# A row normalisation with four unequal buffers and a first tile stored in halves

## Chip, cores, metric

The kernel runs on one core of one Trainium2 chip. The metric is device time in microseconds (us). Each kernel was run several times, and medians, ranges and ratios are of these runs. A ratio is the mean time of one kernel's fast runs over the mean time of the fast runs of the kernel before that were made in the same rounds on the same chip, so it is not quite the ratio of the medians that stand beside it, which are of all runs. A run that lies over 1.5% above the fastest of its kernel counts as slow; there were two, and both were profiled (sizes_only and halves_six).

## The reference

```python
x: (32, 512, 1024) float32
sums = np.sum(np.abs(x), axis=-1, keepdims=True)
return (x / (sums + 1e-8)).astype(np.float32)
```

There are 16,384 rows of 1024 numbers. Each row is read once, summed, scaled and written once: 67.1 MB in and 67.1 MB out.

## The kernel before

The rows are dealt to 128 partitions, 128 rows to each, and moved in tiles of 12 rows a partition (the last has 8). Within a tile the rows of one partition are neighbours in memory, so each partition's part is one contiguous line of 48 KB.

```python
R = 12
BUFS = 4
...
def piece(flat, i):
    a, k = P * sum(rows[:i]), rows[i]
    return flat[a : a + P * k, :].rearrange("(p r) d -> p r d", p=P)

sbuf = ctx.enter_context(tc.tile_pool(name="sbuf", bufs=BUFS))
...
for i, k in enumerate(rows):
    x_tile = sbuf.tile([P, R, d], FP32)
    nc.sync.dma_start(out=x_tile[:, :k, :], in_=piece(x_flat, i))
    normalize(x_tile, 0, k, k // 2)
    nc.scalar.dma_start(out=piece(out_flat, i), in_=x_tile[:, :k, :])
```

`normalize` runs one reduce over all rows on VectorE, two tiny operations, then a multiply of half of the rows on VectorE and an activation for each row of the other half on ScalarE, all in place. SyncE issues the loads and ScalarE the stores. A load waits until the store that used its buffer four tiles earlier has landed.

Of the kernel before, what the change touches and what calls it, by code (L numbers as in the profile page):

```python
# [1 line left out]

# [4 lines left out]

FP32 = mybir.dt.float32
EPS = 1e-8


@with_exitstack
def kernel(
    ctx: ExitStack,
    tc: tile.TileContext,
    x: bass.AP,
    out: bass.AP,
):
    nc = tc.nc
    P = nc.NUM_PARTITIONS  # L20

    x_flat = x.flatten_outer_dims()
    out_flat = out.flatten_outer_dims()
    n, d = x_flat.shape


    R = 12
    BUFS = 4
    per_partition = n // P
    assert n % P == 0  # L30
    rows = [R] * (per_partition // R)
    if per_partition % R:
        rows.append(per_partition % R)

    def piece(flat, i):
        a, k = P * sum(rows[:i]), rows[i]
        return flat[a : a + P * k, :].rearrange("(p r) d -> p r d", p=P)

    sbuf = ctx.enter_context(tc.tile_pool(name="sbuf", bufs=BUFS))
    stats = ctx.enter_context(tc.tile_pool(name="stats", bufs=4))  # L40

    def normalize(x_tile, r0, k, kv):

        s = stats.tile([P, R], FP32)
        nc.vector.tensor_reduce(  # L45
            out=s[:, :k],
            in_=x_tile[:, r0 : r0 + k, :],
            axis=mybir.AxisListType.X,
            op=mybir.AluOpType.add,
            apply_absolute_value=True,  # L50
        )
        nc.vector.tensor_scalar_add(out=s[:, :k], in0=s[:, :k], scalar1=EPS)  # L52
        inv = stats.tile([P, R], FP32)
        nc.vector.reciprocal(out=inv[:, :k], in_=s[:, :k])  # L54
        nc.vector.tensor_mul(  # L55
            out=x_tile[:, r0 : r0 + kv, :],
            in0=x_tile[:, r0 : r0 + kv, :],
            in1=inv[:, :kv].unsqueeze(2).to_broadcast([P, kv, d]),
        )
        for r in range(kv, k):  # L60
            row = x_tile[:, r0 + r, :]
            nc.scalar.activation(  # L62
                out=row,
                in_=row,
                func=mybir.ActivationFunctionType.Copy,
                scale=inv[:, r : r + 1],
            )

    with tc.manual_schedule():
        for i, k in enumerate(rows):  # L70
            x_tile = sbuf.tile([P, R, d], FP32)
            nc.sync.dma_start(out=x_tile[:, :k, :], in_=piece(x_flat, i))  # L72
            normalize(x_tile, 0, k, k // 2)
            nc.scalar.dma_start(out=piece(out_flat, i), in_=x_tile[:, :k, :])  # L74


# [1 line left out]
_INS = ['x']  # L78
_OUTS = [((32, 512, 1024), 'float32')]


# [23 lines left out]
```

## Time and profile before

| | before |
|---|---|
| time, median (range) | 317.77 us (317.46 to 318.05, 6 runs) |
| span of the profiled run | 315.8 us |
| VectorE busy | 212.4 us, 67% |
| mean DMA rate over the span | 425 GB/s |
| rate in the middle | 430 to 437 GB/s |

The kernel is a stream with the DMA as its bound. The page's DMA row and the rate say that; the prediction below shows these lines and reads them. How a DMA's work is split matters later: each transfer is carried by 16 DMA engines, eight lines each. Each line is one packet in the trace, with its start, duration and size. The trace's list of packets doesn't name the engine, but on one engine a packet starts as the last one ends (3 to 4 ns before its end), so most engines can be followed from packet to packet.

### The profile page before, as it was taken

How to read it: one execution, taken by the hardware profiler on the slowest of the kernel's cores; microseconds unless marked ns; L12 is line 12 of the kernel's file. 1: busy time of each engine (PE TensorE's matmuls, PEld its weight loads, DVE VectorE, ACT ScalarE, POOL GpSimd, SP SyncE). 2: the span in 40 equal slices, each digit the busy share in tenths (PEclk: the TensorE clock that was granted, in tenths of full speed). 3: DMA queues.
4: the chain of work that ended last, by engine and by line, in shares of the span. 5: the costliest groups of instructions: out<-in, count | busy, mean ns of one | idle time of the engine just before them, and what ended most of it. 6: DMA issues, size and time to landing. Idle time of an engine off the chain costs nothing.

```text
span 315.8 us, 227 instructions
## 1 busy us (share of the span) xinstructions
DVE 212.4 (67%) x44; ACT 69.0 (22%) x65; POOL 0.2 (0%) x4
## 2 busy tenths in 40 slices
DVE  0069999998499079719944991797099449949300
ACT  0010804308007000700440070007003400701300
POOL 0000000000000000000000000000000000000000
DMA  8999999999999999999999999999999999999996
GB/s 311 467 417 411 467 367 442 405 454 430 417 448 430 423 461 423 436 442 417 442 442 411 449 436 411 448 436 423 448 430 436 442 413 450 421 448 417 448 403 278
DMA packets 3169, 134.23 MB, mean 425 GB/s; under 512 B 352, under 2 KB 352, under 8 KB 352
## 3 DMA queue, kind: packets, MB, share of 16 engines
q1 hardware_dynamic: 1584, 67.11, 49.8%
q10 hardware_dynamic: 1584, 67.11, 49.1%
q14 instruction: 1, 0.01, 0.0%
HBM read 67.11 MB, written 67.11 MB: 425 GB/s over the span
## 4 chain that ended last, share of the span: by engine, by line
DMA 55%; DVE 25%; another core or an unknown queue 9%; ACT 4%; issue 0%; SPq 0%; DVEq 0%; ACTq 0%
DMA x_tile<-in_x_dram 41%; DVE s L45 19%; DMA out_dram<-x_tile 14%; DVE x_tile L55 6%; ACT x_tile L62 4%; DVE inv L54 0%; DVE s L52 0%; SPq L72 0%; DVEq L54 0%; ACTq L74 0%
## 5 line engine op out<-in xcount | busy, mean ns | idle before, releaser
L45 DVE TENSOR_REDUCE s<-x_tile 128x12 f32<-128x12288 f32 (+1 forms) x11 | 138.2, 12564 | 81.1 <-DMA x_tile<-in_x_dram 81.1
L62 ACT ACTIVATE x_tile<-x_tile,inv 128x1024 f32<-128x1024 f32 x64 | 67.7, 1135 | 207.6 <-DVE inv L54 207.6
L55 DVE TENSOR_TENSOR x_tile<-x_tile,inv 128x6144 f32<-128x6144 f32 (+1 forms) x11 | 70.0, 6364 | 0.4
L62 ACT ACT_TABLE_LOAD x1 | 1.3, 1283 | 18.4 <-DMA x_tile<-in_x_dram 18.4
L54 DVE RECIPROCAL inv<-s 128x12 f32<-128x12 f32 (+1 forms) x11 | 2.5, 226 | 0.9
L52 DVE TENSOR_SCALAR s<-s 128x12 f32<-128x12 f32 (+1 forms) x11 | 1.9, 173 | 0.4
L89 POOL MEMSET const-bfloat16-1.0<- 128x1 bf16 x1 | 0.1, 101 | 0.0
L89 POOL MEMSET const-uint8-127<- 128x1 uint8 x1 | 0.1, 101 | 0.0
L89 POOL MEMSET const-float32-0.0<- 128x1 f32 x1 | 0.1, 98 | 0.2 <-issue 0.2
L89 POOL MEMSET const-float32-1.0<- 128x1 f32 x1 | 0.1, 98 | 0.0
## 6 DMA issues: line engine op xcount, KB each, us to landing
x_tile<-in_x_dram SPq DMA_DIRECT2D x10, 6144.0 KB, 38.5
out_dram<-x_tile ACTq DMA_DIRECT2D x10, 6144.0 KB, 53.5
x_tile<-in_x_dram SPq DMA_DIRECT2D x1, 4096.0 KB, 33.7
out_dram<-x_tile ACTq DMA_DIRECT2D x1, 4096.0 KB, 19.5
```

What stands on the lines that cost most here:

```text
L45: nc.vector.tensor_reduce(out=s[:, :k], in_=x_tile[:, r0 : r0 + k, :], axis=mybir.AxisListType.X, op=mybir.AluOpType.add, apply_absolute_v ...
L52: nc.vector.tensor_scalar_add(out=s[:, :k], in0=s[:, :k], scalar1=EPS)
L54: nc.vector.reciprocal(out=inv[:, :k], in_=s[:, :k])
L55: nc.vector.tensor_mul(out=x_tile[:, r0 : r0 + kv, :], in0=x_tile[:, r0 : r0 + kv, :], in1=inv[:, :kv].unsqueeze(2).to_broadcast([P, kv, d]),)
L62: nc.scalar.activation(out=row, in_=row, func=mybir.ActivationFunctionType.Copy, scale=inv[:, r : r + 1],)
L89: nc = _bacc.Bacc("TRN2", target_bir_lowering=False, num_devices=1)
```

## The change

The intent is to keep more bytes in flight (51 rows instead of 48) and to begin storing earlier.

```diff
-    R = 12
-    BUFS = 4
+    R = 16
+    SLOTS = [R, 12, 12, 11]
...
+    while left:
+        rows.append(min(left, SLOTS[len(rows) % len(SLOTS)]))
+        left -= rows[-1]
...
-    sbuf = ctx.enter_context(tc.tile_pool(name="sbuf", bufs=BUFS))
+    slots = [
+        ctx.enter_context(tc.tile_pool(name=f"slot{b}", bufs=1))
+        for b in range(len(SLOTS))
+    ]
...
-            x_tile = sbuf.tile([P, R, d], FP32)
+            x_tile = slots[i % len(SLOTS)].tile([P, SLOTS[i % len(SLOTS)], d], FP32)
             nc.sync.dma_start(out=x_tile[:, :k, :], in_=piece(x_flat, i))
-            normalize(x_tile, 0, k, k // 2)
-            nc.scalar.dma_start(out=piece(out_flat, i), in_=x_tile[:, :k, :])
+            h = k if i else k // 2
+            for r0 in range(0, k, h):
+                normalize(x_tile, r0, h, h // 2)
+                nc.scalar.dma_start(
+                    out=piece(out_flat, i)[:, r0 : r0 + h, :],
+                    in_=x_tile[:, r0 : r0 + h, :],
+                )
```

More of the change, by code (lines that the diff above doesn't have):

```diff
@@ L24 @@
     n, d = x_flat.shape
-    R = 12
-    BUFS = 4
-    per_partition = n // P
+    R = 16
+    SLOTS = [R, 12, 12, 11]
     assert n % P == 0
-    rows = [R] * (per_partition // R)
-    if per_partition % R:
-        rows.append(per_partition % R)
+    left = n // P
+    rows = []
+    while left:
+        rows.append(min(left, SLOTS[len(rows) % len(SLOTS)]))
+        left -= rows[-1]
     def piece(flat, i):
```

## The prediction

> **What bounds the kernel now.** I read the page's slices first, to see which resource is full, then the queues and issues, then stretches of the span, and last the chain of waits and the timeline for the edges. The program is pure streaming: 128 rows of 4096 B in each of 128 partitions, in and out.
>
> ```profile
> DVE 212.4 (67%) x44; ACT 69.0 (22%) x65; POOL 0.2 (0%) x4
> ...
> DMA  8999999999999999999999999999999999999996
> ...
> DMA packets 3169, 134.23 MB, mean 425 GB/s; under 512 B 352, under 2 KB 352, under 8 KB 352
> ...
> x_tile<-in_x_dram SPq DMA_DIRECT2D x10, 6144.0 KB, 38.5
> out_dram<-x_tile ACTq DMA_DIRECT2D x10, 6144.0 KB, 53.5
> x_tile<-in_x_dram SPq DMA_DIRECT2D x1, 4096.0 KB, 33.7
> ```
>
> The DMA row is 9 in 38 of 40 slices; only the first and the last are lower. VectorE is idle for a third of the span. The same by stretches (start:end, length, busy times, clock, DMA share, GB/s):
>
> ```profile
> 0.00:8.00 8.00, 0.00 (x0) 0.00 (x0) 0.20 (x4) 1.00 0.83 307
> ...
> 60.00:80.00 20.00, 18.11 (x4) 6.34 (x6) 0.00 (x0) 1.00 1.01 435
> ...
> 200.00:240.00 40.00, 30.88 (x5) 6.34 (x6) 0.00 (x0) 1.00 1.00 433
> 240.00:280.00 40.00, 28.05 (x8) 12.69 (x12) 0.00 (x0) 1.00 1.00 433
> 280.00:300.00 20.00, 13.48 (x4) 4.27 (x4) 0.00 (x0) 1.00 1.00 435
> 300.00:308.00 8.00, 0.00 (x0) 0.00 (x0) 0.00 (x0) 1.00 0.93 401
> 308.00:316.00 8.00, 0.00 (x0) 0.00 (x0) 0.00 (x0) 1.00 0.63 270
> ```
>
> From 60 to 300 us the rate is 433 to 435 GB/s. 134.2 MB at 433 take 310.0 us, so of the 315.8 us span only 5.8 are not full-rate transfer: about 2.8 at the start (the first 100 us move 42.1 MB, which is 97.2 us' worth) and 3.0 at the end. The measured 317.85 us are 2.0 more than the span. The chain of waits names DMA for 55% and VectorE for 25%, but it follows single tiles; the reduces in it are no bound, because other tiles' transfers fill the DMA meanwhile. These lines of the timeline show it (start, length, engine, and in brackets the idle time before and what ended it):
>
> ```profile
> 18.35 12.95 DVE L45 TENSOR_REDUCE s<-x_tile 128x12 f32<-128x12288 f32 x1 [18.35 <-DMA x_tile<-in_x_dram]
> 38.45 0.37 ACTq L74 DMA_DIRECT2D out_dram<-x_tile  x1
> 58.38 0.34 ACTq L74 DMA_DIRECT2D out_dram<-x_tile  x1
> 83.26 12.95 DVE L45 TENSOR_REDUCE s<-x_tile 128x12 f32<-128x12288 f32 x1 [5.05 <-DMA x_tile<-in_x_dram]
> 112.19 12.95 DVE L45 TENSOR_REDUCE s<-x_tile 128x12 f32<-128x12288 f32 x1 [8.91 <-DMA x_tile<-in_x_dram]
> 257.23 12.95 DVE L45 TENSOR_REDUCE s<-x_tile 128x12 f32<-128x12288 f32 x1 [8.91 <-DMA x_tile<-in_x_dram]
> 281.44 8.69 DVE L45 TENSOR_REDUCE s<-x_tile 128x8 f32<-128x8192 f32 x1 [4.13 <-DMA x_tile<-in_x_dram]
> 295.18 0.34 ACTq L74 DMA_DIRECT2D out_dram<-x_tile  x1
> ```
>
> The first four loads (48 rows) are all issued by 3 us and would alone keep the DMA busy to 2.8 + 48 x 1.211 = 60.9 us (a row of all partitions is 524,288 B, 1.211 us at 433 GB/s). The first store joins at 38.45, so there is no hole before it. At the end, the last load lands at 281.4 and its store is issued at 295.18, but SyncE's closing waits (the stretches 280 to 293 and 293 to 310; us in total, times, longest) show when the two stores before it land:
>
> ```profile
> SPq L100 <- DMA out_dram<-x_tile: 42.5, 1, 42.5
> SPq L100 <- DMA out_dram<-x_tile: 14.5, 1, 14.5
> ```
>
> The first of these waits began after SyncE's last load issue at 247.7, so it ended near 290.3, and the second near 305: older stores cover the last computation, and the last store has some 10 us in hand.
>
> **What the Trainium skill says.** "DMA: Bandwidth & Descriptors", section "Where 436 GB/s comes from", gives 435.2 GB/s as the limit of the ports; the trace's 433 to 435 agrees, so the steady stretch has nothing left. The same page, "Queues, rings and completion order", says that each DMA engine takes turns between its queues, one packet at a time. The trace agrees, and shows what a packet is here: 3169 = 22 transfers x 16 engines x 9 + 1, thus eight data packets (one partition's contiguous rows each) and a small one per engine. The last load has 8-row packets beside stores of 12-row ones: it took 257.2 to 281.4, 24.2 us or 20.0 rows, which is 8 + 12. An equal share of bytes would give 16 rows, 19.4 us. So one load and one store advance in step, packet by packet, and a pair costs the sum of their rows. "VectorE: DVE Perf Modes", section "The perf-mode tier table", has the reduce at one element per cycle at any type; 12,288 elements at the page's 0.96 GHz are an estimated 12.80 us, and 12.95 is measured, so row counts scale its cost linearly.
>
> **The change part by part.** Tiles become 16, 12, 12, 11, 16, 12, 12, 11, 16, 10 rows: 10 instead of 11. Bytes are the same. Buffers hold 51 rows instead of 48. Loads fall from 11 to 10; stores stay at 11, since tile 0 is stored as 8 + 8. VectorE keeps 44 instructions and the same elements; one row costs (12.95-8.69)/4 = 1.066 us in the reduce and (6.56-4.42)/2 = 1.066 in the multiply. From the start of the reduce to the store's issue: 20.1 us for 12 rows (38.45-18.35), 13.7 for 8 (295.18-281.44); worked out from these, 26.5 for 16, 18.8 for 11, 16.9 for 10. Everything hangs on whether the DMA ever has both queues empty, so I walk through it, with data taken to end 1 us before landing (first load: 2.8 + 12 x 1.211 = 17.3 against the landing at 18.33), and 2 us from issue to first byte.
>
> Start. Load 0 now has 16 rows: 2.8 + 19.4, landing at 23.2 instead of 18.3. The first half's store is issued at 23.2 + 13.7 = 36.9, the second at 50.6, tile 1's at 70.6, tile 2's at 90.5. So halving wins 1.5 us against 38.45 for the first store, with 8 rows in it instead of 12: the larger tile eats what the halves give. By 58.4 us the old kernel had offered 24 rows, the new one 16. Loads alone would last to 2.8 + 51 x 1.211 = 64.6, well past 36.9: no hole here either.
>
> Hand-over. The first store of the old kernel needed about 5 us to get its turn; with that, half 0a is moved from about 42 in step with eight load packets (8 + 11.6 rows) to 66, half 0b with load 3's last five (11.9 rows) to 80, then alone to 84. Only then is the 16-row buffer free, and load 4 goes out near 85 (old: 73.7). The load queue is empty from about 80 to 87: the one new wait. But tile 1's store, queued since 70.6, keeps the engines full there. Cost: 0.
>
> Steady part, each pair as the sum of rows x 1.211: load 4 lands near 121, load 5 at 150, load 6 at 179, load 7 at 211, load 8 at 245. Each next load is issued 4 to 6 us before the previous has ended, where the old kernel had 9.6; a late one costs nothing while a store is queued. Stores are issued 12 to 33 us before their turn (store 4 ready at 148, its turn at 172; store 7 ready at 230, its turn at 265). VectorE needs 79 to 85 us per cycle of 51 rows, while the DMA needs 2 x 51 x 1.211 = 123.5. No hole.
>
> End. Load 9 lands near 271; tile 8's 26.5 us end at about the same time, so VectorE is just free. Store 8 is issued at 271.4, when store 7 still has 11 us to go; store 9 at 288.2, when store 8 goes on to 300.5. Both have about 10 us in hand, as before. Last data at 2.8 + 256 x 1.211 = 312.8, plus the old tail.
>
> Sum: removed from the path 0, added 0; the floor of 310.0 + 2.8 + 3.0 + 2.0 stays: 317.8 us.
>
> **Rivals.** (1) The earlier first store and the 51 rows fill holes. For it: slices 4 to 6 waver between 367 and 467 GB/s. Against: the DMA share over 0 to 60 us is 0.99, and with two queues more packets are underway and not yet counted; 16 half packets of 48 KB are 0.4 MB, 0.9 us, which fits the dip. If it were right, at most 1 us: 316.8. (2) The 16-row buffer, held until both halves have landed, starves the DMA near 80 to 87 us. For it: load 4 is some 11 us later. Against: the store of tile 1 is queued. If it came 10 us late there would be up to 7 us of hole: 321 to 325. (3) Sizes: 16-row lines start every 64 KiB in HBM. The page "DMA: Bandwidth & Descriptors", section "Latency and other measured facts", reports less bandwidth at large powers of two as pitch, from 512 KiB up; 64 KiB isn't in its table and no run here shows it. For it: nothing but the round number; against: the 8-row last tile of this kernel (32 KiB) loads in step without loss. If 5% were lost on the 48 rows of 128 in such tiles, 6 us: 324. (4) The end: a 26.5 us tile right before the last one could make the last store late. My walk leaves 10 us and may be off by 3; beyond that each us counts whole.
>
> **Range and chances.** The mechanism gives 317.8; the three runs spread by 0.3. Rival 1 and a smoother tail could take a us, packets of 64 KiB that end less evenly over the engines could add one or two: 316.5 to 319.5. Over 2% faster would be below 311.5, under the floor of full-rate transfer plus both edges: 1%. Slower than 324.2 needs rival 3 at 5% or two others together: 4%. Same: 95%.
>
> **What would show it.** Right: the DMA row stays at 9 between its edges, 433 to 435 GB/s in the middle, first store near 37, second near 51, load 4 issued near 85, last load landing near 271, last store issued near 288. 21 transfers x 144 + 1 = 3025 packets would show that 64 KiB lines stay one packet each. Wrong: a slice below 9 near 80 to 90 (rival 2), a rate below 430 wherever 16-row tiles move (rival 3), or a gap after store 8 at the end (rival 4).

## The result, and the profile after

The changed kernel takes 319.62 us at the median (318.81 to 321.28, 6 runs) against 317.77 (317.46 to 318.05). The ratio is 1.0068, with a 95% interval of 1.0039 to 1.0097: slower by some 2 us, inside 2%, and just outside the predicted range. Its runs also spread over 2.5 us, where the kernel before spreads over 0.6. The profiled run of 320.97 us is one of the slower ones.

The page of the changed kernel, the lines that answer to those shown of before:

```profile
DVE 211.2 (66%) x44; ACT 70.0 (22%) x66; POOL 0.2 (0%) x4
...
DMA  9999999999999999999999999999999999999993
...
DMA packets 3025, 134.23 MB, mean 421 GB/s; under 512 B 336, under 2 KB 336, under 8 KB 336
```

The DMA row is still full in 39 of 40 slices; only the last fell, from 6 to 3. The packets are the predicted 3025, so a line of 64 KiB is one packet. The timeline of the changed kernel:

```profile
22.59 8.69 DVE L50 TENSOR_REDUCE s<-x_tile 128x8 f32<-128x8192 f32 x1 [22.59 <-DMA x_tile<-in_x_dram]
36.27 0.37 ACTq L83 DMA_DIRECT2D out_dram<-x_tile  x1
49.77 0.34 ACTq L83 DMA_DIRECT2D out_dram<-x_tile  x1
123.81 17.22 DVE L50 TENSOR_REDUCE s<-x_tile 128x16 f32<-128x16384 f32 x1 [16.42 <-DMA x_tile<-in_x_dram]
276.24 0.34 ACTq L83 DMA_DIRECT2D out_dram<-x_tile  x1
276.64 10.82 DVE L50 TENSOR_REDUCE s<-x_tile 128x10 f32<-128x10240 f32 x1 [0.49 <-DMA x_tile<-in_x_dram]
293.61 0.34 ACTq L83 DMA_DIRECT2D out_dram<-x_tile  x1
```

The first half's store goes out at 36.3, as worked out. From the fifth load on, landings are late: 123.8 instead of 121, and 276.6 instead of 271 for the last. But the last store, issued at 293.6, still waits for its turn; the DMA has no hole. The two kernels by stretches (start:end, length, busy times, clock, DMA share, GB/s), first the one before, then the changed one:

```profile
100.00:150.00 50.00, 31.98 (x6) 9.41 (x9) 0.00 (x0) 1.00 1.00 433
150.00:200.00 50.00, 31.83 (x9) 12.69 (x12) 0.00 (x0) 1.00 1.01 437
200.00:250.00 50.00, 39.02 (x8) 12.69 (x12) 0.00 (x0) 1.00 0.99 430
...
312.00:314.00 2.00, 0.00 (x0) 0.00 (x0) 0.00 (x0) 1.00 0.38 164
314.00:316.00 2.00, 0.00 (x0) 0.00 (x0) 0.00 (x0) 1.00 0.00 0
```

```profile
100.00:150.00 50.00, 33.23 (x8) 14.71 (x14) 0.00 (x0) 1.00 0.99 429
150.00:200.00 50.00, 37.18 (x9) 9.99 (x11) 0.00 (x0) 1.00 1.00 431
200.00:250.00 50.00, 21.10 (x6) 9.10 (x9) 0.00 (x0) 1.00 1.00 431
...
312.00:314.00 2.00, 0.00 (x0) 0.00 (x0) 0.00 (x0) 1.00 0.57 246
314.00:316.00 2.00, 0.00 (x0) 0.00 (x0) 0.00 (x0) 1.00 0.14 61
316.00:318.00 2.00, 0.00 (x0) 0.00 (x0) 0.00 (x0) 1.00 0.05 20
```

The middle runs at nearly the same rate. The end is drawn out: 20 GB/s over 2 us are 40 KB, the size of one packet of the last store. So only one packet started between 316 and 318 us. The packet list shows a second engine finishing until 316.5; from then on one engine worked and the other fifteen had nothing to do.

The records of single packets say how that engine fell behind. Nearly all packets of one size take the same time to a few ns (48 KB 1.815 us, 64 KiB 2.418, 44 KB 1.665). A few take longer, mostly by 0.2 us or more. I call the excess over the usual time, summed over all packets, stalled time; the usual time is the median of the packets of that size. Worked out from both traces:

| | before | changed |
|---|---|---|
| stalled time, mean of the 16 engines | 2.19 us | 2.89 us |
| of it in packets that start after 60 us | 0.07 us | 1.35 us |
| the sixteen parts of the last store land (mean) | 313.2 to 314.7 (313.8) | 313.7 to 318.0 (314.7) |

The span grew by 3.2 us. The mean engine accounts for 0.9 of that (313.8 to 314.7), and the distance from the mean engine to the last one for 2.4 (0.9 became 3.3). An engine that can be followed through without an idle moment ends at 311.1 us plus its own stalls (up to 311.9 where its first packet starts later). In the kernel before, the first one ends at 312.85 with 1.73 stalled, the last at 314.26 with 3.14. In the changed kernel one ends at 313.33 with 2.26, the last at 317.70 with 6.58. (Of its 16 engines, two couldn't be followed to the end.) The last one stalled nine times, all in loads, near 2, 38, 66, 91, 125, 154, 206, 208 and 269 us; in the kernel before an engine stalls near 2 us, when the first load begins, and near 40 us, when the first store does, and hardly again. In the changed kernel 40 packets stall by over 0.2 us after 60 us. Of these, 14 start between 65.9 and 68.1 us, just after the second half's store has begun to move (64.7), and ten between 90.1 and 90.8 us; these ten are first packets of load 4, after the load queue has been empty (84.1 to 90.1). The other sixteen lie later, on six engines as far as they can be followed.

So the DMA as a whole was as busy as predicted, and the time of this run is set by the slowest of its sixteen engines. What remained to be found is which part of the change makes engines stall.

### The profile page after: what moved, and what is told of

Read it like the earlier page. It is cut to its first block, busy times and chain, and to the rows that moved or that the text cites. A ratio compares the mean times of both kernels' runs of the same rounds, so it can differ in the third digit from the quotient of the medians.

```text
span 319.0 us, 224 instructions
## 1 busy us (share of the span) xinstructions
DVE 211.2 (66%) x44; ACT 70.0 (22%) x66; POOL 0.2 (0%) x4
## 2 busy tenths in 40 slices
DMA packets 3025, 134.23 MB, mean 421 GB/s; under 512 B 336, under 2 KB 336, under 8 KB 336
## 4 chain that ended last, share of the span: by engine, by line
another core or an unknown queue 39%; DMA 32%; DVE 20%; SPq 0%; issue 0%; DVEq 0%; ACTq 0%
DMA x_tile<-in_x_dram 18%; DMA out_dram<-x_tile 14%; DVE s L50 13%; DVE x_tile L60 7%; SPq L77 0%; DVE inv L59 0%; DVE s L57 0%; DVEq L59 0%; ACTq L83 0%
## 5 line engine op out<-in xcount | busy, mean ns | idle before, releaser
L50 DVE TENSOR_REDUCE s<-x_tile 128x12 f32<-128x12288 f32 (+4 forms) x11 | 138.2, 12562 | 80.7 <-DMA x_tile<-in_x_dram 80.7
L67 ACT ACTIVATE x_tile<-x_tile,inv 128x1024 f32<-128x1024 f32 x65 | 68.8, 1135 | 200.7 <-DVE inv L59 200.7
L60 DVE TENSOR_TENSOR x_tile<-x_tile,inv 128x6144 f32<-128x6144 f32 (+3 forms) x11 | 68.9, 6267 | 0.4
L59 DVE RECIPROCAL inv<-s 128x12 f32<-128x12 f32 (+4 forms) x11 | 2.5, 226 | 0.9
L57 DVE TENSOR_SCALAR s<-s 128x12 f32<-128x12 f32 (+4 forms) x11 | 1.9, 173 | 0.4
```

What stands on the lines that cost most here:

```text
L50: nc.vector.tensor_reduce(out=s[:, :k], in_=x_tile[:, r0 : r0 + k, :], axis=mybir.AxisListType.X, op=mybir.AluOpType.add, apply_absolute_v ...
L57: nc.vector.tensor_scalar_add(out=s[:, :k], in0=s[:, :k], scalar1=EPS)
L59: nc.vector.reciprocal(out=inv[:, :k], in_=s[:, :k])
L60: nc.vector.tensor_mul(out=x_tile[:, r0 : r0 + kv, :], in0=x_tile[:, r0 : r0 + kv, :], in1=inv[:, :kv].unsqueeze(2).to_broadcast([P, kv, d]),)
L67: nc.scalar.activation(out=row, in_=row, func=mybir.ActivationFunctionType.Copy, scale=inv[:, r : r + 1],)
```

## The experiments

All runs gave correct results. In the table "stalls" is the mean stalled time of an engine in packets that start after 60 us, and "last store" is when the sixteen parts of the last store land; both are of the profiled run alone, which for sizes_only and halves_six was a slow one.

| run | median (range), us | ratio | stalls | last store |
|---|---|---|---|---|
| changed kernel | 319.62 (318.81 to 321.28) | 1.0068 | 1.35 | 313.7 to 318.0 |
| halves_only | 320.35 (318.29 to 322.62) | 1.0091 | 0.81 | 313.7 to 315.6 |
| sizes_only | 324.17 (322.00 to 327.92) | 1.0194 | 1.76 | 316.6 to 325.0 |
| near_equal | 317.93 (317.73 to 318.24) | 1.0011 | 0.29 | 313.8 to 315.3 |
| three_16 | 329.63 (328.92 to 330.16) | 1.0380 | 0.57 | 327.4 to 327.5 |
| three_12 | 318.91 (318.55 to 319.12) | 1.0036 | 0.26 | 315.7 to 316.3 |
| uneven_48 | 320.64 (320.20 to 322.04) | 1.0101 | 0.38 | 318.3 to 319.1 |
| before_short_lines | 325.31 (325.26 to 325.38) | 1.0240 | 0.01 | 321.9 to 322.6 |
| after_short_lines | 325.76 (325.66 to 325.77) | 1.0253 | 0.01 | 322.1 to 322.7 |
| halves_short_lines | 325.13 (325.08 to 325.24) | 1.0238 | 0.04 | 321.6 to 322.5 |
| sizes_short_lines | 326.17 (326.00 to 326.34) | 1.0270 | 0.01 | 322.4 to 323.1 |
| before_six | 317.44 (317.25 to 317.68) | 0.9999 | 0.02 | 313.7 to 315.0 |
| halves_six | 322.01 (320.46 to 325.45) | 1.0135 | 1.47 | 322.7 to 322.8 |
| mixed_full | 327.29 (326.49 to 330.10) | 1.0324 | 0.47 | 323.6 to 323.8 |
| mixed_eight | 321.78 (321.61 to 322.75) | 1.0139 | 1.04 | 319.9 to 320.0 |
| after_again | 322.10 (one run) | | 1.29 | 313.8 to 319.1 |
| sizes_again | 322.69 (one run) | | 4.04 | 314.1 to 319.7 |

**The two parts singly.** Two kernels each take one part of the change.

```diff
 halves_only
-    R = 16
-    SLOTS = [R, 12, 12, 11]
+    R = 12
+    SLOTS = [R, 12, 12, 12]
 sizes_only
-            h = k if i else k // 2
+            h = k
```

> Four equal buffers of 12 rows as before, only the first tile scaled and stored in halves of 6 rows. Theory S (unequal sizes make load packets stall on some engines, and the engines then end apart): as before, ratio 0.998 to 1.002, the sixteen parts of the last store landing within 1.6 us of each other. Rival H (the two half stores hold the first buffer until both have landed, the load queue runs dry at 83 to 90 us and restarts cold): ratio 1.004 or more, and stalled load packets after 60 us.

> Buffers of 16, 12, 12 and 11 rows, the first tile whole. Theory S: as the changed kernel, ratio 1.005 to 1.009, and the parts of the last store land 3 us or more apart. Rival H: ratio 0.998 to 1.002. Rival E (the end alone: a last tile of 10 rows behind one of 16 instead of 8 behind 12): as the changed kernel, but the landings spread only in the last two stores.

Both parts cost. The sizes alone cost clearly more than both parts together, the halves alone about as much. That sinks theory S for the halves (0.998 to 1.002 expected, 1.0091 measured) and rival H for the sizes. Rival E falls too: in the repeat of sizes_only the second store already lands in parts from 109.5 to 119.0 us (99.9 to 102.6 in the kernel before), long before the end. The costs don't add, so a sum over the parts isn't the way to account for this change. The trace of halves_only is of its fastest run (318.29), 0.8 us over the median of the kernel before; its slower runs, up to 322.62, have no trace, so that their time too is stalled time is not shown. The profile of sizes_only fell on its slowest run (327.92, counted as slow because it lies over 1.5% above the fastest), in which one engine had stalled 13.1 us. I don't rest on it; the repeat at 322.69 us is read further down.

**Nearly equal buffers, and large equal buffers.**

```diff
 near_equal                              three_16
-    R = 16                              -    R = 16
-    SLOTS = [R, 12, 12, 11]             -    SLOTS = [R, 12, 12, 11]
+    R = 13                              +    R = 16
+    SLOTS = [R, 13, 13, 12]             +    SLOTS = [R, 16, 16]
-            h = k if i else k // 2      -            h = k if i else k // 2
+            h = k                       +            h = k
```

> Buffers of 13, 13, 13 and 12 rows: again 51 rows, nearly equal, the first tile whole. Theory S: ratio 0.998 to 1.003. If the 51 rows themselves (fewer, larger transfers) cost the time: 1.005 or more.

> Three equal buffers of 16 rows, all lines 64 KiB, the first tile whole. Theory S: no stalled load packets once the stores have begun, load packets at their usual 2.418 us; the total may still grow by up to 4 us, because the last tile's 26.5 us of computation are covered by about 23 us of stores only. Rival P (16-row lines at a 64 KiB pitch transfer worse): load packets over 2.45 us throughout, the rate in the middle under 430 GB/s, ratio above 1.015.

The same 51 rows in nearly equal buffers cost some 0.1%, with an interval of 0.9999 to 1.0024: neither the 51 rows nor fewer, larger transfers are the trouble. In three_16 the 64 KiB packets take 2.418 us at the median, load or store, which is the same rate as 48 KB in 1.815. That refutes rival P. The run is 12 us slower all the same, and for another reason than any engine's lag. Its last stretches and the lines around the last tile:

```profile
290.00:300.00 10.00, 9.84 (x4) 2.06 (x2) 0.00 (x0) 1.00 0.30 131
300.00:306.00 6.00, 6.00 (x1) 6.00 (x7) 0.00 (x0) 1.00 0.00 0
306.00:310.00 4.00, 0.69 (x1) 0.37 (x1) 0.00 (x0) 1.00 0.61 262
```

```profile
280.19 17.22 DVE L50 TENSOR_REDUCE s<-x_tile 128x16 f32<-128x16384 f32 x1 [12.81 <-DMA x_tile<-in_x_dram]
306.78 0.34 ACTq L83 DMA_DIRECT2D out_dram<-x_tile  x1
```

From 300 to 306 us no byte moves while VectorE works: this is what a hole looks like, and why the prediction looked for one. The last load landed at 280.2, its computation took 26.6 us, and older stores covered it only to 297. I had expected the stores to last longer, hence up to 4 us instead of 12.

**A dry load queue, and unequal buffers without one.**

```diff
 three_12 (on the kernel before)         uneven_48 (on the changed kernel)
-    BUFS = 4                            -    R = 16
+    BUFS = 3                            -    SLOTS = [R, 12, 12, 11]
                                         +    R = 14
                                         +    SLOTS = [10, 12, R, 12]
                                         -            h = k if i else k // 2
                                         +            h = k
```

> Three equal buffers of 12 rows, otherwise the kernel before. The load queue must run dry, since the fourth load waits for the first store. Theory U (load and store lines of different length, taken in turn, push single DMA engines out of step, and these stall most): no stalled load packets beyond the start, the first store and the 8-row end, the sixteen parts of the last store within 2 us; up to 3 us of hole at the end as the last computation of 13.7 us has fewer stores to cover it, so ratio 1.000 to 1.012. Rival V (each dry load queue restarts cold and stalls): stalls of 0.3 us or more on most engines at every load from the fourth on, ratio over 1.015.

> Buffers of 10, 12, 14 and 12 rows: 48 rows as before, unequal neighbours, small one first so that the load queue isn't dry; no halves. Theory U: ratio 1.004 to 1.015, and the last store's parts 2.5 us or more apart. Rival V: ratio 0.998 to 1.002.

With three buffers the load queue does run dry (for 14.5 us before the fourth load), and the stalls don't come: 0.26 us after 60 us, nearly all of it in stores after 280 us, and none in the first packets of that load. The 0.36% fits holes of up to 2.3 us in all before the last two stores. Rival V as stated is refuted: a dry queue alone doesn't stall. In the changed kernel, though, the restart near 90 us is one of the two moments at which many engines do. Uneven_48 costs 1.0%, as U had it. Its last store lands within 0.8 us, which U had not, but the store before it lands from 301.2 to 307.0 us: one engine had stalled 6.8 us, and the other fifteen, out of work at the end, waited 4.4 to 5.1 us for it.

**Lines of one row.** The transfers are unchanged but for which row lies in which partition, so that each packet is one row of 4 KiB in every kernel. The same edit was made on the kernel before, on the changed one, and on each part alone.

```diff
-        return flat[a : a + P * k, :].rearrange("(p r) d -> p r d", p=P)
+        return flat[a : a + P * k, :].rearrange("(r p) d -> p r d", p=P)
```

> The changed kernel, but the rows of a tile are dealt out so that every partition's line is one row of 4 KiB, so packets of all tiles are equally long. Theory U: the difference to the same edit of the kernel before is within 0.2%, and the engines end within 1.5 us of each other. If the sizes of the buffers cost time by themselves: 0.5% or more over the same edit of the kernel before.

> The kernel before with lines of one row, the partner of the run ahead of it. Shorter packets may cost a little rate; an estimate from the 9 ns that the smallest packets take in the trace is 8 x 9 ns per 48 KB line, 4%, at worst: ratio 1.00 to 1.04.

> Four equal buffers, the first tile in halves, lines of one row. If half stores only disturb through unequal lines: within 0.3% of the kernel before with such lines (1.024). Rival O, from the run with lines of 6 rows: an early store gets more turns and the loads fall behind for good, so the last load lands later and its computation leaves a hole at the end: 1 us or more over that.

> The unequal buffers without halves, lines of one row. Theory U: within 0.3% of the kernel before with such lines (which was 1.024), where whole lines cost 1.9%; a hole at the end of up to 3 us may come on top.

The edit itself costs 2.4%: a 4 KiB packet takes 159 ns, where an eighth of a 32 KiB packet (1213 ns) is 152, and the rate in the middle is 422 GB/s instead of 433. But it takes the stalls away in every kernel, and with them nearly all that the change costs. Dividing the ratios of the table, the changed kernel stands at 1.0253/1.0240 = 1.0013 of its partner instead of 1.0068, the halves alone at 0.9998 instead of 1.0091, the sizes alone at 1.0029 instead of 1.0194. (The last two were run on another chip than the partner, each beside the kernel before.) The run-to-run range falls to 0.1 us for the changed kernel. The ends of the kernel before and the changed one with such lines:

```profile
318.00:320.00 2.00, 0.00 (x0) 0.00 (x0) 0.00 (x0) 1.00 1.01 418
320.00:326.00 6.00, 0.00 (x0) 0.00 (x0) 0.00 (x0) 1.00 0.31 125
```

```profile
318.00:320.00 2.00, 0.00 (x0) 0.00 (x0) 0.00 (x0) 1.00 1.02 422
320.00:326.00 6.00, 0.00 (x0) 0.00 (x0) 0.00 (x0) 1.00 0.33 136
```

Both run full until they stop; the drawn-out end is gone. This shows that the buffers' sizes, the halves, the dry load queue and the order of work by themselves cost the changed kernel next to nothing. Their cost comes with the stalls, and after 60 us the stalls come only with the longer lines. The edit also changes which addresses an engine moves one after the other; no run parts that from the length of the lines.

**Equal lines that are long.** Short lines are equal and short at once. Two pairs were to part these. In the first every line has 6 rows (4 in the last tile), in the second 8.

```diff
 before_six, halves_six (from halves_only)
-        return flat[a : a + P * k, :].rearrange("(p r) d -> p r d", p=P)
+        n = 6 if k % 6 == 0 else 4
+        t = flat[a : a + P * k, :]
+        return t.rearrange("(g p n) d -> p g n d", p=P, n=n)
 (and the tile's side of each transfer cut alike)

 mixed_full
-    SLOTS = [R, 12, 12, 11]
+    SLOTS = [8, R, R, 8]
-            h = k if i else k // 2
+            h = k
 mixed_eight: as mixed_full, and
-        return flat[a : a + P * k, :].rearrange("(p r) d -> p r d", p=P)
+        t = flat[a : a + P * k, :]
+        return t.rearrange("(g p n) d -> p g n d", p=P, n=8)
```

> Four buffers of 12 rows with the first tile in halves of 6, and every transfer cut into lines of 6 rows (the last tile of 8 into lines of 4), so that the half stores and the loads they alternate with have equal lines. Theory U: the same time as its partner without halves to 0.3%, all runs within 0.8 us, no stalled load packets from 60 us on. If halving itself costs (the buffer held for two stores, the dry load queue): 0.6% or more over the partner.

> The kernel before with lines of 6 rows, the partner of the run ahead. Twice as many packets, 176 more on each engine; at the 9 ns of fixed time per packet that the 4 KiB lines showed (159 ns against an eighth of the 32 KiB line's 1213 ns), an estimated 1.6 us more: ratio 1.003 to 1.007.

> Buffers of 8, 16, 16 and 8 rows, 48 in all, whole lines of 8 or 16 rows, no halves. Theory U: stalled packets in the middle, on some engines twice as long in all as on others, ratio 1.004 or more. The 26.5 us of the last 16-row tile may leave a hole at the end as well; it is to be told apart in the trace (no engine has a packet then).

> The same buffers, every transfer cut into lines of 8 rows, so all packets of the program are 32 KB. Theory U (it is the inequality of the lines, not their number or the buffers): stalls at the start and the first store only, at most 2.5 us for each engine, engines within 2 us of each other at the end; ratio 0.998 to 1.004, plus a hole at the end if there is one. Rival B (unequal buffers stall whatever the lines): stalls as in the run with whole lines.

Theory U in its strict form falls here. Mixed_eight, whose profiled run was fast, has equal lines and more stalled time than mixed_full (1.04 against 0.47 us, of which 0.76 fall between 120 and 140 us, on all engines). Halves_six has equal lines and is 322.01/317.44 = 1.014 of its partner; its trace has 1.47 us of stalls, nearly all in stores, and in its next-to-last transfers one engine ends up 5 us and more behind the rest, but that trace is of its slowest run, which counts as slow (325.45). Equal lines of 32 KB don't protect, and those of 24 KB didn't in the one run traced.

In both pairs a hole at the end weighs more than the stalls, so the ratios can't be read as the price of stalling. In mixed_full all engines but one are idle for 8.5 to 10.5 us before 294 us, in mixed_eight those that can be followed for 3.7 to 5.9. In halves_six the hole has two causes worth knowing. Its issues, and the last tile:

```profile
x_tile<-in_x_dram SPq DMA_DIRECT2D x10, 6144.0 KB, 59.0
out_dram<-x_tile ACTq DMA_DIRECT2D x9, 6144.0 KB, 39.2
```

```profile
297.56 8.69 DVE L52 TENSOR_REDUCE s<-x_tile 128x8 f32<-128x8192 f32 x1 [6.56 <-DMA x_tile<-in_x_dram]
311.57 0.38 ACTq L85 DMA_DIRECT2D out_dram<-x_tile  x1
```

In the kernel before a load takes 38.5 us to land and a store 53.5; here it is 59.0 and 39.2. The likely reason is that stores that got early turns left the buffers waiting in the load queue instead of the store queue, and that it stays so, because from then on one store makes room for one load. The last load lands at 297.6 instead of 281.4 us, and too few stores are left to cover its computation. But 14 of this load's 16 parts had landed by 291.5: the stalls of the two slowest engines added the last 6 us. Rival O was formed from this run. Its shift of the queues is there in the fast run of halves_short_lines too (a load takes 60.0 us to land against 42.0 in before_short_lines, a store 39.0 against 55.5, and the last load lands at 293.0 instead of 284.1), yet without a hole or a cost: the store before the last lands until 312.6, and the last one is issued at 307.0.

Before_six was expected at 1.003 to 1.007 and came out at 0.9999: its stalls in all are 1.53 us an engine instead of 2.19, which gives back 0.7 of the estimated 1.6 us for twice as many packets. The rest is in the estimate, which counted whole durations although packets overlap by 3 to 4 ns: from 60 to 260 us the 4 KiB packets follow each other at 155.4 ns on one engine, so a packet costs an estimated 5 ns and 176 of them 0.8 us. In the middle before_six runs at 433 GB/s, like the kernel before.

**Second traces.**

> The changed kernel once more, for a second trace. Theory U: again one or two engines alone have twice the stalled time of the rest, and the end follows the worst of them: the last engine's end is 311.1 us plus its stalls to 0.2 us.

> Unequal buffers without halves once more, for a second trace. Theory U: one engine far behind again, by 3 us or more, in both the loads and the stores it takes part in, and a hole near 281 to 285 us on the other engines, which wait for the last but one tile.

The changed kernel again has two engines apart, with 7.58 and 6.64 us stalled where the others that could be followed have 2.2 to 3.2. The last one ends at 318.82, and 311.1 + 7.58 is 318.7. Sizes_again is not as expected: no single straggler and no hole, but eleven engines with 6.1 to 8.0 us of stalls and five with 2.8 to 4.2, in loads and in stores, many of them between 50 and 95 us. There the rate shows it, too (sizes_again):

```profile
60.00:100.00 40.00, 39.79 (x9) 12.69 (x12) 0.00 (x0) 1.00 1.01 402
...
314.00:316.00 2.00, 0.00 (x0) 0.00 (x0) 0.00 (x0) 1.00 0.66 287
316.00:318.00 2.00, 0.00 (x0) 0.00 (x0) 0.00 (x0) 1.00 0.57 246
```

The share stays at 1.01 while the rate falls to 402 GB/s: a stalled packet counts as busy. So how many engines stall differs from run to run; that the spread of the times comes from it is likely, but only these runs are traced. Both second traces are single runs, so their state is unknown.

No version beat the kernel before. Before_six ties with it.

## Why the prediction was wrong

The predicted 317.8 us is 1.8 us under the median, and the range ended at 319.5.

- **The bound and the floor** held. The bytes move at 429 to 431 GB/s in the middle, against 430 to 437 before.
- **Start and hand-over** held for the DMA's work: first stores at 36.3 and 49.8 us (36.9 and 50.6 worked out). The halves win nothing there, as argued, and the load queue's dry spell is covered by a store. What the prediction didn't foresee is that 24 packets stall at this hand-over.
- **Steady part**: the landings came 3 to 6 us later than in the walk, from load 4 at 123.8 (121) to load 9 at 276.6 (271). Load 4 is late as a whole: its first packet moves at 90.1 instead of 87. The rest is lag of single engines: the walk treated 16 engines as one, but a transfer lands with its slowest part, and load 9's parts land from 272.3 to 276.6.
- **End**: no hole in the changed kernel, as worked out, though some 5 us later. That rival 4 is a real danger is seen in three_16.
- **The step that failed** is "Sum: removed from the path 0, added 0; the floor of 310.0 + 2.8 + 3.0 + 2.0 stays". The term of 3.0 for the end was carried over unchanged. The remark in the range that packets "end less evenly over the engines could add one or two" named the right place, but gave the wrong reason (64 KiB) and too small a size. Measured in the profiled run: the mean engine ends 0.9 us later and the last one another 2.4 us after it, 3.3 instead of 0 to 2. At the median the whole time grew by 1.85. The 64 KiB packets are not to blame, as three_16's 2.418 us show; halves_only has no packet over 48 KB and loses 0.9%.
- **Rivals**: 1 gained nothing, 2 and 4 didn't come about, and 3 was wrong.

What is shown: in both traces of the changed kernel (runs of 320.97 and 322.10 us, both slower than its median) the extra time is the stalled time of the slowest DMA engines; each part of the change causes such stalls by itself; with lines of one row the stalls and nearly all of the difference vanish. What stays open is why a packet of a long line stalls, and whether length or the order of addresses matters. Unequal lines are neither needed (halves_six and mixed_eight stall with equal ones) nor enough to stall most engines (mixed_full). Runs of whole-tile transfers in equal or nearly equal buffers stall least (0.02 to 0.57 us after 60 us); uneven_48 and mixed_full have no more in the mean, but in uneven_48 two thirds of it sit on one engine. The traces name no engines, so whether the same ones always lag couldn't be seen.

## What to carry to other kernels

When the DMA row is full from end to end, a change of buffers has only the edges to win, here under 6 us, and can lose by making the sixteen engines end apart; look at the last few us of the stretches, where a share of a few hundredths means one engine working alone. Equal buffers and whole-tile transfers kept the engines together here, and 4 KiB lines did so in every kernel, at 2.4% in rate. Ask at the end of a stream how many us of older stores are queued when the last load lands, and keep that above the last tile's computation.

## What the Trainium skill lacked or had wrong

- "DMA: Bandwidth & Descriptors", "Queues, rings and completion order", has engines take turns by packets and agrees with the pairing seen here. The page has slow engines beside iDMA traffic and on the software path, but not in a plain stream of loads and stores such as this one: 6.58 us of stalls on the slowest engine, which set the time, where the quickest that could be followed had 1.85 and all had the same bytes.
- No page has a measured price of a line's length from 4 to 64 KiB. Packets took 159 ns for 4 KiB, 1213 for 32 KiB and 2418 for 64 KiB, which fits about 8 ns a packet, of which 3 to 4 overlap with the packet before; lines of 4 KiB ran at 422 GB/s where 48 KB lines ran at 433, and cost 2.4% of the time.
- "DMA: Bandwidth & Descriptors", "Latency and other measured facts", lists loss at large powers of two in row pitch from 512 KiB up. At a pitch of 64 KiB there was none: 2.418 us for 65,536 B is 27.1 GB/s an engine, as for 49,152 B in 1.815 us.
- No page that was read for this case says that the DMA share counts stalled packets as busy: 402 GB/s at a share of 1.01 in sizes_again, against 434 at 1.00 in the kernel before from 60 to 100 us.
